# Three ways of feeding TensorE in the gate and up products of a decoder layer: 144-token halves, alternating PSUM tiles, and 256 + 32 tokens

## Chip, cores and metric

The kernel runs on one core of a Trainium2 chip. The metric is the device time of one execution in microseconds (us); lower is better. Two runs of the kernel before gave 2517.14 and 2518.53 us, median 2517.84 us.

## The reference, cut to what matters

One inference step of a decoder layer is computed for a prompt of 256 tokens and for 8 samples of 4 tokens, so 288 tokens go through the same weights. The layer is a half-step feed-forward network (FFN), a mixing stage (a state space model and sparse attention), and a second half-step FFN. Only the first FFN is changed:

```
def _swiglu(x, w_gate, w_up, w_down):
    return (jax.nn.silu(x @ w_gate) * (x @ w_up)) @ w_down
...
x_p = x_p + FFN_RES * _swiglu(_rms_norm(x_p, p['ffn1_norm']), p['ffn1_w_gate'], p['ffn1_w_up'], p['ffn1_w_down'])
```

The model width is 2048 (16 blocks of 128) and the FFN width 5632 (44 blocks of 128). Weights and inputs are float32.

## The kernel before

All activations are kept as tiles of 128 features by 288 tokens. To keep float32's accuracy with single-pass products, every operand is split into an upper part, rounded to the type float32r, and a lower part, the rest, in float32r too. A product of weights and activations is then three matmuls that add up in the same PSUM tile: upper weights by upper activations, upper weights by lower activations, and lower weights by upper activations. The profile prints both types as "f32".

`project` (L221) computes 256 columns of a weight matrix against all 288 tokens. `fetch` (L204) brings in a piece of 512 rows by 256 columns by a DMA on the SP queue into `raw` (4 buffers); `parts` (L211) makes `whi` on ScalarE (L216) and `wlo` on VectorE (L217), 3 buffers each. For each of the two blocks of 128 weight columns there is one PSUM tile, and the loops are: piece of 4 row blocks, then column block j, then row block k, then the three matmuls.

```
            for j in range(m):
                ...
                for k in range(kt):
                    ...
                    nc.tensor.matmul(out, wh, xh, start=k0 + k == 0, stop=False)
                    nc.tensor.matmul(out, wh, xl, start=False, stop=False)
                    nc.tensor.matmul(out, wl, xh, start=False, stop=k0 + k == K - 1)
                    if k % 2:
                        self.tick()
```

These three are L240, L241 and L242. The first matmul operand is the stationary one (the weights in the array), the second streams through it. In every row of these lines in the profile, a LDWEIGHTS on "PEld" goes with a MATMUL on "PE". PSUM tiles come by turns from two pools, so one project's tiles are called `psy` and the next one's `acc`; `hh` and `hl` are the upper and lower parts of the scaled input x, `hi` and `lo` those of the gated product that the down projection takes.

`swiglu` (L340) goes through the FFN width in six groups of 8, 8, 8, 8, 6 and 6 blocks. In a group, `project` is called for gate and for up, two blocks at a time (L359); each resulting PSUM tile is multiplied by 1/rms on VectorE (L372), gate goes through Silu on ScalarE (L374), and gate and up are multiplied and split again (L352, L250). Then 8 calls make the down projection of the group (L380), which VectorE adds to x (L384). A group of 8 blocks has 8 calls for gate and up. Each has 16 row blocks, 2 column blocks and 3 matmuls: 768 matmuls in all.

The order of the instructions on TensorE is that of the program, written by hand. The other engines' orders are made by a scheduler with priorities. Work beside the products (`prepare`, the state space model's matrices) is written as generators that go on a step at each `tick`; in the first FFN its small matmuls and its VectorE work lie among the products of the first four groups. VectorE has both this work and L217 in its queue.

Of the kernel before, what the change touches and what calls it, by code (L numbers as in the profile page):

```python
# [10 lines left out]
F32 = mybir.dt.float32  # L11
# [4 lines left out]
AL = mybir.AluOpType  # L16
AX = mybir.AxisListType

P = 128
SEQ, DB, DT = 256, 8, 4  # L20
# [13 lines left out]
CT = 4  # L34
# [22 lines left out]
def constants():  # L57
    """What depends on the shapes alone."""
    f32 = np.float32
    pos = np.concatenate([np.arange(SEQ), np.tile(PAST + np.arange(DT), DB)]).astype(f32)  # L60

    def rope(rot):
        half = rot // 2
        f = (500000.0 ** (-np.arange(half, dtype=np.float64) * 2.0 / rot)).astype(f32)
        ang = (pos[None, :] * f[:, None]).astype(f32).astype(np.float64)
        c, s = np.cos(ang).astype(f32), np.sin(ang).astype(f32)
        return np.concatenate([c, c]), np.concatenate([-s, s])

    cq, sq = rope(HD // 4)
    ci, si = rope(ID // 4)  # L70
    rope_i = np.zeros((P, 2, NT), f32)
    rope_i[:, 0] = 1.0
    for o in (0, ID):
        rope_i[o:o + ID // 4, 0], rope_i[o:o + ID // 4, 1] = ci, si
    t = np.arange(P)
    causal = np.where(t[None, :] <= t[:, None], 0.0, NEG).astype(f32)
    b, j = np.divmod(np.arange(DB * DT), DT)
    new = np.where((b[:, None] == b[None, :]) & (j[None, :] <= j[:, None]), 0.0, NEG).astype(f32)
    rows = np.zeros((4, DB * DT, 2, 4, 4, HEADS, DT), f32)
    for i in range(DB * DT):  # L80
        for n in range(4):
            rows[n, i, b[i] // 4, n, b[i] % 4, :, j[i]] = 1.0
    strip = np.arange(P) // 32
    same = np.arange(P)[:, None] % 32 == np.arange(P)[None, :] % 32
    strips = np.stack([same, same & (strip[:, None] < strip[None, :])], 1).astype(f32)
    sign = np.where(np.arange(P) // 16 % 2 == 0, 1.0, -1.0).astype(f32)
    pick = np.zeros((P, 34), f32)
    pick[:, 2] = 1.0
    return {
        "c_rope_q": np.stack([cq, sq], 1),  # L90
        "c_rope_i": rope_i,
        "c_causal": causal,
        "c_new": new,
        "c_wmask": (j[:, None] == np.arange(DT)[None, :]).astype(f32),
        "c_rows": rows.reshape(P, 2, 4, P),
        "c_strips": strips,
        "c_sign": sign[:, None],
        "c_pick": pick,
        "c_part": (np.arange(P) % 16).astype(f32)[:, None],
    }  # L100


class Late:
    """A list whose items are made when they are first asked for."""
# [14 lines left out]
class Net:  # L119
# [57 lines left out]
    def pipe(self, n, every, *stages):  # L177
        """n items, one each `every` ticks, through stages (ticks behind the first, what to do)."""
        for t in range((n - 1) * every + max(lag for lag, _ in stages) + 1):
            for lag, fn in stages[::-1]:  # L180
                i, odd = divmod(t - lag, every)
                if not odd and 0 <= i < n:
                    fn(i)
            yield
# [18 lines left out]

    def fetch(self, src, kt, n):  # L204
        """[128 kt, n] of a matrix in DRAM."""
        raw = self.wp.tile([P, 4, 256], F32, tag="raw", bufs=4, name=self.name("raw"))[:, :kt, :n]
        with self.tc.high_priority(offset=FIRST):
            self.nc.sync.dma_start(raw, src.rearrange("(c p) n -> p c n", p=P))
        return raw

    def parts(self, raw):  # L211
        """Its upper and its lower parts."""
# [8 lines left out]
    def project(self, w, c0, n, xs):  # L221
        """PSUM tiles of w[:, c0:c0+n]^T x, of 128 columns of w each (n <= 256)."""
# [23 lines left out]

    def split(self, src):
        nc = self.nc
        hi, lo = self.t(F32R, "hi"), self.t(F32R, "lo")
        nc.scalar.copy(hi, src)  # L250
        nc.vector.tensor_tensor(lo, src, hi.bitcast(F32), op=AL.subtract)
        return hi, lo

# [1 line left out]

    def load_x(self, xp, xs):
        """The inputs, turned as they are asked for."""
# [27 lines left out]
    def rows(self, pool, src):  # L285
        """[n, 128] in DRAM, to be turned."""
# [4 lines left out]
    def turned(self, pool, row, n):  # L291
        """[n, 128] -> [128, n]"""
# [7 lines left out]
    def rsqrt(self, out, m, s):  # L300
        """out = m ** -0.5, the table's root refined by a Newton step; s is scratch."""
# [8 lines left out]
    def normed(self, g):  # L310
        """gain * x, split, and a function that gives the broadcast 1 / rms."""
# [28 lines left out]
    def swiglu(self, pool, i, g, done):  # L340
        nc = self.nc
# [4 lines left out]
        for n in (8, 8, 8, 8, 6, 6):  # L346
# [8 lines left out]
            for j in range(n // 2):  # L355
                c0 = (f0 + 2 * j) * P
                a = []
                for w in (wg, wu):
                    for p in self.project(w, c0, 256, hs):  # L359
# [55 lines left out]

    def exp(self, pool, x, shape):
        """e ** x to float32's accuracy"""
        nc = self.nc
        T = lambda dt=F32: pool.tile(shape, dt, name=self.name("ex"))  # noqa: E731
# [15 lines left out]
    def cos_sin(self, pool, a, shape):  # L435
        nc = self.nc
        T = lambda: pool.tile(shape, F32, name=self.name("cs"))  # noqa: E731
# [19 lines left out]
        # the quadrant, -2 to 2  # L457
# [24 lines left out]
    def prepare(self):  # L482
        """Constants; the SSM's discretization, its matrices and rotations."""
# [12 lines left out]
        dram = lambda name, shape: self.dram.tile(shape, F32, name=name)  # noqa: E731  # L496
# [13 lines left out]
        mul = lambda o, a, b: nc.vector.tensor_tensor(o, a, b, op=AL.mult)  # noqa: E731  # L510
        add = lambda o, a, b: nc.vector.tensor_tensor(o, a, b, op=AL.add)  # noqa: E731
        sub = lambda o, a, b: nc.vector.tensor_tensor(o, a, b, op=AL.subtract)  # noqa: E731

        def states(a):
            """[n, 128] of states, by their parts: [part][n, 4, 16]"""
# [3 lines left out]
        with ExitStack() as outer:  # L519
# [15 lines left out]
            # partition (page, sixteenth of it): where that begins in the caches  # L535
# [11 lines left out]
            # each state's two parts, 16 states a time: [groups, (4, part, 16)]  # L547
            S = [GR, P]
            T = lambda: pool.tile(S, F32, name=self.name("pz"))  # noqa: E731
# [37 lines left out]
            K = lambda shape: keep.tile(shape, F32, name=self.name("pk"))  # noqa: E731  # L587
# [7 lines left out]
            # from here the second factors have their sign by part  # L595
            for a in (sT, fiT):
                nc.vector.tensor_scalar(a, a, sign, None, op0=AL.mult)
            # e ** (i theta n), n a power of two, kept on the unit circle
# [19 lines left out]
            # the decay's powers, 0 to CT, from the first and from the last  # L618
# [19 lines left out]
            # the state that comes in, and that with the decay of a chunk  # L638
# [12 lines left out]
            # b_bar: [states, group, channel]  # L651
# [5 lines left out]
            # c: [(group, channel), states], the imaginary part negative  # L657
# [14 lines left out]
            for c8 in range(8):  # L672
# [16 lines left out]
                def powers(a, a_s, fr, fi, n, op, what):  # L689
                    """[states, group, power, channel]"""  # L690
# [20 lines left out]
                # e ** (i theta CT n)  # L711
# [18 lines left out]
                # what comes out of what comes in 0 to CT - 1 tokens later  # L730
# [13 lines left out]

    def zproj(self, c0, n, hs, scaled=True, tag="t", bufs=N_T):
        """Projections of the normed x, as SBUF tiles of 128 features; not scaled: 1 / rms is still to come."""
# [20 lines left out]
    def chunks(self, z, a):  # L767
        """u: what is left is [channel, place in a chunk, chunk], the samples' chunks first"""
# [5 lines left out]
    def ssm(self, pool, u, za, every):  # L774
        """The state space model: a chunk's inputs to its last state and to its own outputs, a scan of the chunks' states
        (rotated to where the decay is real), and each chunk's outputs from the state before it; four groups a time."""
# [4 lines left out]
        # inputs by group, in zeros where its neighbour's are  # L781
# [43 lines left out]
        def into(n):  # L825
# [16 lines left out]
            flat = lambda a: a.rearrange("p g c -> p (g c)")  # noqa: E731  # L842
# [38 lines left out]
        # the states at the ends  # L881
# [26 lines left out]
    def pages(self, pool, src, i, b, n, tag, bufs):  # L908
        """A sixteenth of a page a partition."""
# [5 lines left out]
    def select(self, qi, kw):  # L915
        """The indexer's inputs; then, for the samples, the bias of the keys each query may see:
        a quarter of the cache in each 32 partitions."""
        nc, D = self.nc, self.D
        with self.tc.tile_pool(name="sel", bufs=1) as pool:
# [24 lines left out]
            # qi is not scaled by 1 / rms: its head weights are instead  # L944
# [5 lines left out]
            # head weights as columns: [(half h t), (half b t)] for each sequence  # L950
# [67 lines left out]
            # the n-th largest of a row, a bit at a time (from the sign down)  # L1018
            one = lambda n, dt=F32: pool.tile([P, 1], dt, name=n)  # noqa: E731
# [19 lines left out]
            # of the equal ones the first: as many as are missing  # L1039
# [9 lines left out]
    def prompt(self, z, out):  # L1049
        """The prompt's selection and attention; the norms of q and k."""  # L1050
# [36 lines left out]
        # head h's sum of squares in partition 32 (h % 4) + h // 4  # L1087
# [76 lines left out]
    def by_token(self, pair, key):  # L1164
        """The two heads of k or v by token, to the outputs too."""
# [18 lines left out]
    def sample(self, z, out):  # L1184
# [4 lines left out]
        with self.tc.tile_pool(name="sample", bufs=1) as pool:  # L1189
# [8 lines left out]
            # queries by sequence, each kv head's in zeros  # L1198
            for h in range(HEADS):
                nc.scalar.copy(qz[:, h // REP, :, h * DT:(h + 1) * DT], q[h][:, SEQ:NT].rearrange("p (b t) -> p b t", t=DT))  # L1200
            for x in range(2):
                # columns: [eighth of the sixteenths, (page, sixteenth)], then the new keys
# [199 lines left out]
```

## Time and profile before

| what | value |
| --- | --- |
| median of the two runs | 2517.84 us |
| span of the profiled execution, first to last instruction | 2517.2 us |
| TensorE's mean granted clock in it (1 is full speed) | 0.999 |
| matmuls, and weight loads, each | 18917 |

The profiled execution's span lies within 0.7 us of the median, so what is outside the span is below a thousandth. In the timelines a MATMUL's duration reaches to its modelled end and overlaps the next one's; the distance from one start to the next is what an instruction costs in a stream. The same holds for LDWEIGHTS. A row of windows gives a stretch and its length, then busy us and number of instructions of PE, PEld, DVE (VectorE), ACT (ScalarE) and POOL (of PE alone where only PE was asked for), then TensorE's granted clock, the DMA engines' busy share and GB/s. In a list of groups the busy us and mean ns stand behind the bar, then the idle time ahead of them and what ended it.

### The profile page before, as it was taken

To read this page: it belongs to the slowest core of one execution; us is meant where nothing else is said; L and a number is where in the kernel's file an instruction comes from. 1 tells how busy PE (TensorE), PEld (TensorE's weight loads), DVE (VectorE), ACT (ScalarE), POOL (GpSimd) and SP (SyncE) were. 2 spreads that over 40 slices of the span, in tenths; PEclk is the share of its full clock that TensorE was granted. 3 is DMA by queue.
4 is the path that set the end of the run, shared out by engine and by line. 5 is a ranking of instruction groups with operands and counts; after the bars stand their busy time and mean duration, and the time that the engine had idled before them with its cause. 6 is when DMAs were issued, how large, how long until landed. Compare 5 with 4: busy or idle time off the path is not lost.

```text
span 2517.2 us, 46484 instructions
## 1 busy us (share of the span) xinstructions
PE 2496.1 (99%) x18917; PEld 2446.9 (97%) x18917; DVE 1529.7 (61%) x2878; ACT 1082.8 (43%) x1600; POOL 98.4 (4%) x116
## 2 busy tenths in 40 slices
PE   8999999999999999999999999999999999999999
PEld 7999999999999998999998999999999999999999
DVE  6658888875555656679644457556555555554555
ACT  5433333333333445445865544344333333333333
POOL 1001000000000000000023210000000000000000
PEclk9999999999999999999999999999999999999999
DMA  6556566565545655446567576555555555555553
GB/s 196 160 160 162 183 195 190 187 184 193 163 154 179 196 170 168 126 133 189 157 216 230 189 244 200 193 167 168 164 164 167 168 168 167 164 166 167 162 174 130
DMA packets 439834, 441.35 MB, mean 175 GB/s; under 512 B 36778, under 2 KB 428964, under 8 KB 439620
## 3 DMA queue, kind: packets, MB, share of 16 engines
q1 hardware_dynamic: 428064, 414.56, 52.3%
q0 software_dynamic: 6688, 20.26, 2.7%
q10 hardware_dynamic: 4868, 3.57, 0.5%
q8 instruction: 148, 2.42, 0.4%
q14 instruction: 66, 0.54, 0.1%
HBM read 418.48 MB, written 19.83 MB: 174 GB/s over the span
## 4 chain that ended last, share of the span: by engine, by line
PE 96%; DMA 1%; DVE 1%; issue 0%; POOL 0%; ACT 0%; POOLq 0%; SPq 0%; ACTq 0%; DVEq 0%
PE acc L240 17%; PE acc L241 17%; PE acc L242 17%; PE psy L240 13%; PE psy L241 13%; PE psy L242 13%; PE aux L1061 1%; PE psy L829 1%; PE aux L1218 1%; PE aux L276 0%; DMA cn<-in_ssm_c_re 0%; DVE wlo L217 0%; PE psy L858 0%; PE aux L1264 0%; PE psy L859 0%
## 5 line engine op out<-in xcount | busy, mean ns | idle before, releaser
L217 DVE TENSOR_TENSOR wlo<-raw,whi 128x1024 fp32r<-128x1024 f32 (+1 forms) x740 | 885.3, 1197 | 754.6 <-ACT whi L216 731.5
L216 ACT CAST whi<-raw 128x1024 fp32r<-128x1024 f32 (+1 forms) x740 | 760.5, 1028 | 1144.4 <-PE acc L241 470.8
L240 PE MATMUL acc<-hh,whi 128*128 128x288 f32 x2240 | 680.3, 304 | 0.0
L242 PE MATMUL acc<-hh,wlo 128*128 128x288 f32 x2240 | 660.6, 295 | 3.1 <-DVE wlo L217 3.1
L241 PE MATMUL acc<-hl,whi 128*128 128x288 f32 x2240 | 661.7, 295 | 0.0
L240 PE MATMUL psy<-hh,whi 128*128 128x288 f32 (+1 forms) x1552 | 465.4, 300 | 0.5 <-DVE g L372 0.3
L241 PE MATMUL psy<-hl,whi 128*128 128x288 f32 (+1 forms) x1552 | 459.5, 296 | 1.2 <-DVE hl L317 1.2
L242 PE MATMUL psy<-hh,wlo 128*128 128x288 f32 (+1 forms) x1552 | 458.6, 295 | 0.0
L240 PEld LDWEIGHTS acc<-hh,whi 128*128 128x128 f32 x2240 | 421.7, 188 | 13.9 <-issue 11.5
L242 PEld LDWEIGHTS acc<-hh,wlo 128*128 128x128 f32 x2240 | 421.8, 188 | 3.6 <-DVE wlo L217 3.6
L241 PEld LDWEIGHTS acc<-hl,whi 128*128 128x128 f32 x2240 | 422.6, 189 | 1.3 <-issue 1.0
L240 PEld LDWEIGHTS psy<-hh,whi 128*128 128x128 f32 (+1 forms) x1552 | 292.2, 188 | 5.5 <-issue 3.9
L241 PEld LDWEIGHTS psy<-hl,whi 128*128 128x128 f32 (+1 forms) x1552 | 293.1, 189 | 2.5 <-DVE hl L317 1.4
L240 PE MATMUL psy<-hi,whi 128*128 128x288 f32 x992 | 293.3, 296 | 0.0
L240 PE MATMUL acc<-hi,whi 128*128 128x288 f32 x992 | 293.3, 296 | 0.0
L241 PE MATMUL acc<-lo,whi 128*128 128x288 f32 x992 | 292.7, 295 | 0.0
L241 PE MATMUL psy<-lo,whi 128*128 128x288 f32 x992 | 292.6, 295 | 0.0
L242 PEld LDWEIGHTS psy<-hh,wlo 128*128 128x128 f32 (+1 forms) x1552 | 292.6, 189 | 0.0
L242 PE MATMUL acc<-hi,wlo 128*128 128x288 f32 x992 | 292.4, 295 | 0.0
L242 PE MATMUL psy<-hi,wlo 128*128 128x288 f32 x992 | 292.3, 295 | 0.0
L240 PEld LDWEIGHTS acc<-hi,whi 128*128 128x128 f32 x992 | 186.3, 188 | 1.4 <-issue 1.2
L240 PEld LDWEIGHTS psy<-hi,whi 128*128 128x128 f32 x992 | 186.3, 188 | 0.7 <-issue 0.4
(403 smaller groups left out, 2351.2 us busy)
## 6 DMA issues: line engine op xcount, KB each, us to landing
raw<-in_ffn_w_gate SPq DMA_DIRECT2D x176, 512.0 KB
raw<-in_ffn_w_up SPq DMA_DIRECT2D x176, 512.0 KB
raw<-in_ffn_w_down SPq DMA_DIRECT2D x160, 512.0 KB
raw<-in_w_in SPq DMA_DIRECT2D x120, 512.0 KB
raw<-in_w_out SPq DMA_DIRECT2D x32, 512.0 KB
raw<-in_ffn_w_down SPq DMA_DIRECT2D x32, 256.0 KB
raw<-in_w_branch_a SPq DMA_DIRECT2D x16, 512.0 KB
raw<-in_w_branch_b SPq DMA_DIRECT2D x16, 512.0 KB
```

The lines of the kernel that those rows point to most:

```text
L216: self.nc.scalar.copy(hi, raw)
L217: self.nc.vector.tensor_tensor(lo, raw, hi.bitcast(F32), op=AL.subtract)
L240: nc.tensor.matmul(out, wh, xh, start=k0 + k == 0, stop=False)
L241: nc.tensor.matmul(out, wh, xl, start=False, stop=False)
L242: nc.tensor.matmul(out, wl, xh, start=False, stop=k0 + k == K - 1)
L829: nc.tensor.matmul(p[:, j * M:(j + 1) * M], I[n][:, j // 2], U[n % 3][:, j // 2, j % 2], start=j == 0, stop=j == 3)
L1061: nc.tensor.matmul(p[:, :L], qi[h // 2][o:o + 64, i * P:(i + 1) * P], kd[o:o + 64, :L], start=True, stop=True)
L1218: nc.tensor.transpose(pk[:, (2 * g + j) * P:(2 * g + j + 1) * P], kr[b4][:, c:c + P], self.ident)
```

## The change

In the first FFN, three of the six groups (blocks 8 to 15, 16 to 23 and 24 to 31, called the second, third and fourth group here) use other forms for gate and up. The second FFN, the down projections and the other groups stay as they are.

- Second group: every matmul is cut in two, tokens 0 to 143 and 144 to 287, with the same stationary operand and into the same PSUM tile.
- Third group: the loop over the two column blocks is the innermost one, so that consecutive matmuls go to the two PSUM tiles by turns and have different weights. The number and shapes of the matmuls stay.
- Fourth group: cut as in the second, but into 256 and 32 tokens.

The rest of the diff removes comments and docstrings.

```
+    def project_cut(self, w, c0, n, xs, cuts):
...
+        for k0 in range(0, K, 4):
+            raw = self.fetch(w[k0 * P:(k0 + 4) * P, c0:c0 + n], 4, n)
+            hi, lo = self.parts(raw)
+            for j in range(2):
+                for k in range(4):
+                    xh, xl = xs[k0 + k]
+                    wh, wl = hi[:, k, j * P:j * P + P], lo[:, k, j * P:j * P + P]
+                    for i, (a, b) in enumerate(((wh, xh), (wh, xl), (wl, xh))):
+                        for c in cuts:
+                            nc.tensor.matmul(acc[j][:, c], a, b[:, c], start=k0 + k + i + c.start == 0,
+                                             stop=k0 + k == K - 1 and i == 2 and c.stop == NT)
+                    if k % 2:
+                        self.tick()
+        return acc
+
+    def project_both(self, w, c0, n, xs):
...
+            for k in range(4):
+                xh, xl = xs[k0 + k]
+                for i, (a, b) in enumerate(((hi, xh), (hi, xl), (lo, xh))):
+                    for j in range(2):
+                        nc.tensor.matmul(acc[j][:, :NT], a[:, k, j * P:j * P + P], b, start=k0 + k + i == 0,
+                                         stop=k0 + k == K - 1 and i == 2)
+                self.tick()
+        return acc
...
                 for w in (wg, wu):
-                    for p in self.project(w, c0, 256, hs):
+                    halves = [slice(0, NT // 2), slice(NT // 2, NT)]
+                    if f0 == 8 and number == 1:
+                        ps = self.project_cut(w, c0, 256, hs, halves)
+                    elif f0 == 16 and number == 1:
+                        ps = self.project_both(w, c0, 256, hs)
+                    elif f0 == 24 and number == 1:
+                        ps = self.project_cut(w, c0, 256, hs, [slice(0, SEQ), slice(SEQ, NT)])
+                    else:
+                        ps = self.project(w, c0, 256, hs)
+                    for p in ps:
```

In `project_cut` and `project_both` the lines ahead of the loops (the turn of the PSUM pools) are as in `project`.

## Rows read from the trace of the kernel before

**Rows 1.** The page: busy us of each engine (part 1), shares of the last chain (part 4).
```profile
PE 2496.1 (99%) x18917; PEld 2446.9 (97%) x18917; DVE 1529.7 (61%) x2878; ACT 1082.8 (43%) x1600; POOL 98.4 (4%) x116
...
PE 96%; DMA 1%; DVE 1%; issue 0%; POOL 0%; ACT 0%; POOLq 0%; SPq 0%; ACTq 0%; DVEq 0%
```

**Rows 2.** Windows: gate and up of the second, third, fourth and fifth group.
```profile
181.29:288.24 106.95, 105.27 (x780) 103.88 (x779) 85.28 (x252) 38.77 (x46) 8.38 (x11) 1.00 0.60 168
342.61:450.20 107.59, 107.59 (x833) 106.79 (x832) 85.98 (x214) 42.23 (x52) 1.46 (x3) 1.00 0.63 192
503.05:608.61 105.56, 105.56 (x811) 105.03 (x810) 71.13 (x152) 41.10 (x50) 4.87 (x6) 1.00 0.63 193
659.84:736.70 76.86, 76.86 (x578) 76.86 (x577) 37.69 (x45) 28.91 (x35) 0.00 (x0) 1.00 0.50 160
```

**Rows 3.** Waits of TensorE, 181 to 609 us: us in total, times, longest.
```profile
PE acc L242 <- DVE wlo L217: 1.7, 1, 1.7
```

**Rows 4.** Page, part 5: weight loads of two lines that share their weights.
```profile
L240 PEld LDWEIGHTS acc<-hh,whi 128*128 128x128 f32 x2240 | 421.7, 188 | 13.9 <-issue 11.5
...
L241 PEld LDWEIGHTS acc<-hl,whi 128*128 128x128 f32 x2240 | 422.6, 189 | 1.3 <-issue 1.0
```

**Rows 5.** Timeline of PEld behind a wait of TensorE: start us, duration us.
```profile
256.25 0.19 PEld L242 LDWEIGHTS acc<-hh,wlo 128*128 128x128 f32 x1 [1.92 <-DVE wlo L217]
256.36 0.19 PEld L240 LDWEIGHTS acc<-hh,whi 128*128 128x128 f32 x1
256.50 0.19 PEld L241 LDWEIGHTS acc<-hl,whi 128*128 128x128 f32 x1
```

**Rows 6.** Timeline of PEld at L829: eight loads, 72 columns streamed by each matmul.
```profile
1035.65 0.97 PEld L829 LDWEIGHTS psy<-U,in 128*128 128x128 f32 x8
1036.54 0.19 PEld L240 LDWEIGHTS acc<-hh,whi 128*128 128x128 f32 x1
```

**Rows 7.** Timeline of PEld at L1235: four loads, 32 columns streamed by each matmul.
```profile
1322.15 0.54 PEld L1235 LDWEIGHTS aux<-z,qz 128*128 128x128 f32 x4
1322.61 0.19 PEld L240 LDWEIGHTS acc<-hh,whi 128*128 128x128 f32 x1
```

**Rows 8.** Timeline of PE, 80 weight columns: first and last of 42 matmuls, and the next.
```profile
942.63 0.30 PE L240 MATMUL psy<-hh,whi 128*80 128x288 f32 x1
...
948.04 0.29 PE L242 MATMUL psy<-hh,wlo 128*80 128x288 f32 x1
948.17 0.29 PE L240 MATMUL acc<-hh,whi 128*128 128x288 f32 x1
```

**Rows 9.** Timeline of PE in the fourth group's stream: first and last of 32 matmuls.
```profile
599.79 0.30 PE L240 MATMUL acc<-hh,whi 128*128 128x288 f32 x1
...
603.92 0.29 PE L241 MATMUL acc<-hl,whi 128*128 128x288 f32 x1
```

**Rows 10.** Timeline of PEld at L1156, plain float32 operands, 256 columns streamed.
```profile
1261.12 0.75 PEld L1156 LDWEIGHTS aux<-pt,vt 128*128 128x128 f32 x4
1261.90 0.19 PEld L240 LDWEIGHTS acc<-hh,whi 128*128 128x128 f32 x1
1262.12 0.19 PEld L241 LDWEIGHTS acc<-hl,whi 128*128 128x128 f32 x1
```

**Rows 11.** Windows of PE alone, around a wait of TensorE for a DMA.
```profile
1373.00:1376.40 3.40, 3.40 (x25) 1.00 0.90 257
1376.40:1379.80 3.40, 1.14 (x10) 1.00 0.84 273
1379.80:1383.20 3.40, 3.40 (x18) 0.51 0.86 304
```

**Rows 12.** Timeline of PE at the lower clock: two consecutive matmuls.
```profile
1382.16 0.44 PE L240 MATMUL acc<-hh,whi 128*128 128x288 f32 x1
1382.40 0.44 PE L241 MATMUL acc<-hl,whi 128*128 128x288 f32 x1
```

More of the change, by code (lines that the diff above doesn't have):

```diff
@@ L245, in project @@
         return acc
+    def project_cut(self, w, c0, n, xs, cuts):
+        nc = self.nc
+        K = len(xs)
+        self.turn = self.wide and not self.turn
+        acc = [self.py() if self.turn else self.ps() for _ in range(2)]
+        for k0 in range(0, K, 4):
[13 more added lines that the diff above has]
+    def project_both(self, w, c0, n, xs):
+        nc = self.nc
+        K = len(xs)
+        self.turn = self.wide and not self.turn
+        acc = [self.py() if self.turn else self.ps() for _ in range(2)]
+        for k0 in range(0, K, 4):
+            raw = self.fetch(w[k0 * P:(k0 + 4) * P, c0:c0 + n], 4, n)
+            hi, lo = self.parts(raw)
+            for k in range(4):
[6 more added lines that the diff above has]
+        return acc
     def split(self, src):
@@ L340, in swiglu @@
     def swiglu(self, pool, i, g, done):
+        number = i
         nc = self.nc
```

## The prediction, made before the changed kernel ran

> **What bounds the kernel now.** I read the page first. TensorE is busy for 2496.1 of 2517.2 us, and 96% of the chain that ended last is TensorE's own work; VectorE, the next engine, has 61% [rows 1]. So a change of the matmul stream counts at full price, unless it fills or opens a wait. Next I read the three changed stretches by windows, and the fifth group beside them [rows 2]. The clock is at full speed, 2.4 GHz, in all four. In the fifth group nothing else lies among the products: 576 matmuls take 76.86 us, which is 133.4 ns for one. At that rate 768 take 102.5 us; the changed groups take 106.95, 107.59 and 105.56 us, so 3.1 to 5.1 us of each is side work and waits. Of waits the list has one over half a microsecond there: 1.7 us in the second group, for `wlo` from VectorE [rows 3], which is busy for 85.28 of 106.95 us in that group.
>
> The question is then what makes up the 133.4 ns. Three readings answer most of it.
> - A weight load is paid for by every matmul. L240 and L241 use the same part of `whi`, one right behind the other, and each has as many loads as the other [rows 4]. Nothing here skips a load because the weights are already in the array. Both halves of a cut matmul will load the same 128 columns again.
> - A load of 128 columns takes about 111 ns, and the next one can't start earlier. Behind the wait, the second load starts 0.11 us after the first, when the array had nothing to stream [rows 5]. At L829 eight loads with only 72 columns streamed by each take 1036.54 - 1035.65 = 0.89 us, so 111 ns each [rows 6]; at L1235, with 32 columns, four take 0.46 us, 115 ns each, of which the first still stands behind a stream of its predecessor [rows 7].
> - The load is not what sets 133.4 ns: with 80 weight columns in place of 128, 41 distances make 5.41 us, 132 ns [rows 8], the same as the 31 distances of 133 ns with 128 columns [rows 9]. So 288 columns streamed set it, and today's load hides under them with 20 ns to spare.
>
> **The change, part by part.** The second group's halves stream 144 columns each. By share that is 67 ns, shorter than the load. The two matmuls and two loads then cost two loads, 2 x 111 = 222 ns, where one matmul cost 133.4. L829 is the nearest row: float32 weights of 128 columns and 72 columns streamed. It is plain float32, whose columns cost more, as rows 10 show (0.22 us for 256), so 72 of them stream for some 61 ns, much like 144 here. Group two: 768 x (222 - 133.4) = +68.0 us. From below, two loads at 109 ns give +65 us. From above, nothing in the trace runs pairs of load and matmul faster than 133.4 ns for more than a handful, so 2 x 133.4 is the far end: +102.5 us. I take 111 ns, from the row nearest in shape.
>
> The fourth group's 256 tokens stream for 133.4 x 256 / 288 = 118.6 ns, which hides the load for the 32 that follow. The 32 tokens then stream for some 15 ns, and the load for the next 256 starts only when the 32 are in the array: 111 ns. Together 229.6 ns; 768 x (229.6 - 133.4) = +73.9 us. The bounds are +65 (both at 109 ns) and +102.5 us.
>
> The third group has as many loads and matmuls of the same shapes as before, in other order. A change of PSUM tile occurs in the trace too: the step from a `psy` tile to an `acc` tile takes 0.13 us like all its neighbours [rows 8], so neither a gain nor a cost is seen. It can't gain more than 768 x (133.4 - 120) = 10.3 us, since 288 columns at 2.4 GHz take 120 ns, and the same row's rounding, 0.14 us, would be a loss of 5 us. I take 0. `wlo` is asked for by the fifth matmul of a piece in place of the third, which is later and so safe; both PSUM tiles end together, which is 12 matmuls or 1.6 us later for the first of them, and the down projection asks for the last gated pair only 30 matmuls on, some 4 us. If that cover fails, it costs about 1 us once.
>
> The rest is free or small. The DMAs, `whi`, `wlo` and the evacuations are as many as before, and the same ticks lie between the same pieces, so the side work keeps its places. Both slower groups give VectorE and the DMA queue more time: the 1.7 us wait should go, -1.7 us. The 1536 additional matmuls and loads wait for nothing and nobody waits for them alone. No engine becomes late next: VectorE's 85 us lie in some 173 us then.
>
> Sum: 68.0 + 73.9 + 0 - 1.7 = +140.2 us on the profiled span of 2517.2, so 2657.4 us. The median of the runs lies 0.7 us above the span: **2658 us**, 5.6% slower. About 2% is what a measurement of this kernel tells from no change.
>
> **The rivals.**
> - *The weights stay, or their load costs no time* (the side that is not slower). If a second load of the weights that are already there were hidden, two halves would cost their columns, 2 x 67 = 133.4 ns, and 256 + 32 the same; the change would be nothing but 768 matmuls more per group. At 13.4 ns each, the whole of what 133.4 is above 120, that is +21 us: 2516 to 2537 us. It decides if a repeated load takes under 133.4 / 2 = 67 ns. Rows 4 count such loads without telling their time, since a 288-column stream covers them; rows 6 and 7 are against it, though with other weights each time. Chance 0.06. The Trainium skill's "TensorE: Matmul & The Clock Gate", section "Back-to-back issue gap", has a rule by which a warm matmul of N columns takes N / 2.4 + 2.5 ns. By that rule a half takes 62.5 ns, the change gives back some 8 ns a pair and the time is 2503 us. Where it can be held against this trace it is low: 122.5 ns for 288 columns, and the rows have 133.
> - *TensorE's issue sets the pace.* If a pair of load and matmul can't be issued in less than today's 133.4 ns over a long stretch, two halves cost 266.8 ns and so do 256 + 32: +205 us, 2721 us. For it: the runs at less are short, eight pairs in rows 6 and four in rows 7. Against it: behind the 1.7 us wait, in which instructions had time to queue, the matmuls go on at the same distance [rows 5], and 80-column weights change nothing. Chance 0.11. [...]
> - *Short float32r streams fall to the price of plain float32.* A plain float32 product is two instructions: the four at L1156 are two products of the program. One with 256 columns takes 1262.12 - 1261.90 = 0.22 us, 0.85 ns a column [rows 10], since a load starts as the matmul ahead of it does. A half would then take 2 x 122 = 245 ns, the pair 489, +273 us; the 32 tokens two loads, 222 ns, the pair 341, +159 us: in all some 2950 us. For it: the trace has no float32r matmul under 256 columns. Against it: the 288-column ones stay far under plain float32's price, and nothing in rows 8 or 9 hints at a second mode. Chance 0.09.
> - *The clock falls.* With loads as the bound, the array streams for only some 60% of the second group. The clock fell once in the trace, behind 3.4 us of which TensorE was busy for 1.14 [rows 11], and 288 columns took 0.24 us then [rows 12]. At half clock a pair of halves takes 240 ns if loads keep their pace (+82 us, within the range) and 444 if they don't (+239 us, the time 2829 or more). A long stretch bound by loads is not in the trace. Chance of the latter 0.03.
>
> **How the numbers follow.** The forecast, loads at 109 to 120 ns in both cut groups, has 0.66; the rivals have 0.06, 0.11, 0.09 and 0.03, and 0.05 is left for what I don't see, most of it slower. The range takes in the bounds of the forecast and the issue rival. Low: 2517.8 + 65 + 65 - 10.3 - 1.7 = 2636. High: 2517.8 + 205 + 5 = 2728. Outside lie the kept weights, plain float32 and the fallen clock, 0.18. Under 2467 us, faster by 2%, none of the cases comes: 0.01. Within 2% is the first rival alone, 0.06; slower has 0.93.
>
> **What would show it.** Windows of the second group should have about 173 us, the third 107.6 and the fourth 179, at clock 1.00. In the second group's timeline loads should start every 0.11 us; in the fourth the distances should alternate between 0.12 and 0.11. TensorE should have 1536 more of both kinds, and no new waits. Distances of 0.07 would speak for the first rival, 0.13 in both halves for issue, 0.24 for plain float32 or the clock, which the windows' clock column tells apart. If the third group moves by more than 10 us, my reading of the PSUM tiles is wrong.

## The result, and the profile after

The changed kernel takes 2659.57 us (2658.11 to 2661.03, two runs), 1.0563 times the time before, with a 95% interval of 1.0546 to 1.058. The forecast was 2658 us, range 2636 to 2728.

First the page of the changed kernel, engines and last chain, against [rows 1]:

```profile
PE 2639.8 (99%) x20453; PEld 2591.6 (98%) x20453; DVE 1535.3 (58%) x2878; ACT 1084.0 (41%) x1600; POOL 96.5 (4%) x116
...
PE 98%; DMA 1%; DVE 1%; issue 0%; ACT 0%; SPq 0%; ACTq 0%; DVEq 0%
```

There are 1536 more matmuls and 1536 more loads, and TensorE has the chain even more to itself. Next the windows of the second, third, fourth and fifth group's gate and up, which answer to [rows 2]:

```profile
180.90:354.56 173.66, 173.66 (x1548) 172.94 (x1547) 89.78 (x255) 39.72 (x47) 8.39 (x11) 1.00 0.38 108
408.96:516.93 107.97, 107.97 (x833) 107.16 (x832) 85.25 (x212) 42.10 (x53) 1.45 (x3) 1.00 0.64 192
570.02:749.87 179.85, 179.85 (x1580) 179.57 (x1578) 74.17 (x152) 42.03 (x52) 4.12 (x6) 1.00 0.38 116
800.71:877.59 76.88, 76.88 (x578) 76.88 (x577) 37.67 (x45) 28.86 (x35) 0.00 (x0) 1.00 0.51 161
```

The whole result is in the second column. The halves take 173.66 us in place of 106.95 (+66.7), the 256 + 32 tokens 179.85 in place of 105.56 (+74.3), the PSUM tiles by turns 107.97 in place of 107.59 (+0.4), and the unchanged fifth group 76.88 in place of 76.86. Together that is +141.4 us; the span grew by 2656.3 - 2517.2 = 139.1. The 2.3 us between lie outside these windows, and only part of them is traced: a wait in the mixing stage for gathered keys is 1.1 us long where it was 2.3, and a second wait for `wlo`, of 1.4 us and ahead of the second group, is gone. Against that, TensorE ran at half clock for a few us twice, from 34 and from 1123 us, and in the kernel before once, from 1380 us. The wait of [rows 3] for `wlo` is gone: the second group's TensorE is busy for all of its 173.66 us, where 1.7 were missing. VectorE's work is nearly the same (89.78 us busy in place of 85.28), and the DMA engines' work is spread thinner (share 0.38 in place of 0.60).

The pace itself is in the timeline of PEld in the second group, loads merged by two:

```profile
249.89 0.30 PEld L262 LDWEIGHTS acc<-hh,whi 128*128 128x128 f32 x2
250.12 0.30 PEld L262 LDWEIGHTS acc<-hl,whi 128*128 128x128 f32 x2
250.34 0.30 PEld L262 LDWEIGHTS acc<-hh,wlo 128*128 128x128 f32 x2
```

Two loads start every 0.22 to 0.23 us, 111 ns each, one behind the other as at L829 in [rows 6]: TensorE loads all the time. In the fourth group, timelines of PE and of PEld:

```profile
649.84 0.38 PE L262 MATMUL acc<-hh,wlo 128*128 128x256 f32 x2
650.07 0.38 PE L262 MATMUL acc<-hh,whi 128*128 128x256 f32 x2
```

```profile
649.81 0.30 PEld L262 LDWEIGHTS acc<-hh,wlo 128*128 128x128 f32 x2
650.04 0.30 PEld L262 LDWEIGHTS acc<-hh,whi 128*128 128x128 f32 x2
650.27 0.30 PEld L262 LDWEIGHTS acc<-hl,whi 128*128 128x128 f32 x2
```

A pair takes 0.23 us (650.07 - 649.84, 650.27 - 650.04). The merged rows also say where inside it the second one starts: a load's record lasts 0.19 us, two end 0.30 us after the first began, so the second began 0.11 us in and the next pair 0.12 us later.

### The profile page after: what moved, and what is told of

Same layout as the page of the kernel before. It is cut to its first block, busy times and chain, and to the rows that moved or that the text cites. A ratio compares the mean times of both kernels' runs of the same rounds, so it can differ in the third digit from the quotient of the medians.

```text
span 2656.3 us, 49552 instructions
## 1 busy us (share of the span) xinstructions
PE 2639.8 (99%) x20453; PEld 2591.6 (98%) x20453; DVE 1535.3 (58%) x2878; ACT 1084.0 (41%) x1600; POOL 96.5 (4%) x116
## 4 chain that ended last, share of the span: by engine, by line
PE 98%; DMA 1%; DVE 1%; issue 0%; ACT 0%; SPq 0%; ACTq 0%; DVEq 0%
PE acc L240 14%; PE acc L241 14%; PE acc L242 14%; PE psy L240 11%; PE psy L241 11%; PE psy L242 11%; PE psy L262 7%; PE acc L262 7%; PE acc L281 2%; PE psy L281 2%; PE aux L1110 1%; PE psy L878 1%; PE aux L1267 0%; PE psy L907 0%; PE psy L908 0%
## 5 line engine op out<-in xcount | busy, mean ns | idle before, releaser
L240 PE MATMUL acc<-hh,whi 128*128 128x288 f32 x1856 | 566.3, 305 | 0.0
L241 PE MATMUL acc<-hl,whi 128*128 128x288 f32 x1856 | 548.2, 295 | 0.0
L242 PE MATMUL acc<-hh,wlo 128*128 128x288 f32 x1856 | 547.0, 295 | 0.0
L240 PEld LDWEIGHTS acc<-hh,whi 128*128 128x128 f32 x1856 | 349.4, 188 | 13.5 <-issue 11.5
L241 PEld LDWEIGHTS acc<-hl,whi 128*128 128x128 f32 x1856 | 350.5, 189 | 1.5 <-issue 1.1
L240 PE MATMUL psy<-hh,whi 128*128 128x288 f32 (+1 forms) x1168 | 351.1, 301 | 0.5 <-DVE g L421 0.3
L242 PEld LDWEIGHTS acc<-hh,wlo 128*128 128x128 f32 x1856 | 349.6, 188 | 0.0
L241 PE MATMUL psy<-hl,whi 128*128 128x288 f32 (+1 forms) x1168 | 346.3, 296 | 1.5 <-DVE hl L356 1.5
L242 PE MATMUL psy<-hh,wlo 128*128 128x288 f32 (+1 forms) x1168 | 345.7, 296 | 0.0
L241 PEld LDWEIGHTS psy<-lo,whi 128*128 128x128 f32 x992 | 186.7, 188 | 0.2 <-DVE lo L290 0.2
```

## Experiments

**The theory:** every matmul loads its weights anew, a load of 128 float32r columns takes 111 ns, and a matmul costs the longer of its own stream and the load for the next one. The rivals differ in what the 111 ns hang on: a floor of short matmuls or of issuing (1), the streamed columns (2), loading the same weights again (3), the PSUM tile (4). Kernels were run once with a profile, beside one run or more of the kernel before on the same chip, which took 2514 to 2522 us; the fourth was timed in rounds. All changes are in gate and up of the first FFN unless said otherwise.

### Fewer weight columns

```
+    m = P if k0 + k + i == 0 or k0 + k + i == K + 1 else cols
+    for c in cuts:
+        nc.tensor.matmul(acc[j][:m, c], a[:, k, j * P:j * P + m], b[:, c], ...)
...
 second group: cuts [0:144, 144:288], cols 64
 third group:  cuts [0:288], cols 64
 fourth group: cuts [0:96, 96:192, 192:288], cols 32
```

> Leaves out: in the second, third and fourth group of the first FFN all products but the first and the last of a PSUM tile use only the first 64 (fourth group: 32) of a block's 128 weight columns, so most of the upper rows of these tiles are missing. Second group: halves of 144 tokens by 64 weight columns. Third: all 288 tokens by 64 weight columns. Fourth: thirds of 96 tokens by 32 weight columns. Theory (a matmul waits for its own weight load, priced by the weight columns, 111 ns for 128): the loads take some 56 and 28 ns and hide again, the streams set the pace at 0.42 to 0.46 ns a column. Second group 1536 x 67 to 73 ns, 106 to 116 us; third 107 to 108 us; fourth 2304 x 45 to 53 ns, 106 to 126 us. Rival 1 (111 ns is a floor of any short float32r matmul, or of issuing a load and a matmul, whatever the weights): second group 174 us, third 108, fourth 2304 x 111 ns, 259 us.

The run took 2527.45 us. Windows of the three groups:

```profile
180.70:291.58 110.88, 109.30 (x1549) 108.21 (x1547) 85.40 (x253) 38.80 (x47) 8.38 (x11) 1.00 0.59 163
347.55:453.65 106.10, 106.10 (x833) 105.13 (x832) 85.57 (x214) 42.10 (x52) 1.46 (x3) 1.00 0.65 195
506.49:620.05 113.56, 113.56 (x2348) 113.22 (x2346) 70.97 (x151) 41.30 (x51) 4.54 (x6) 1.00 0.58 180
```

and the timelines of PE within the second and the fourth:

```profile
239.83 0.30 PE L261 MATMUL psy<-hh,wlo 128*64 128x144 f32 x2
239.96 0.30 PE L261 MATMUL psy<-hh,whi 128*64 128x144 f32 x2
240.10 0.29 PE L261 MATMUL psy<-hl,whi 128*64 128x144 f32 x2
240.23 0.30 PE L261 MATMUL psy<-hh,wlo 128*64 128x144 f32 x2
```

```profile
559.86 0.30 PE L261 MATMUL acc<-hl,whi 128*32 128x96 f32 x3
560.00 0.30 PE L261 MATMUL acc<-hh,wlo 128*32 128x96 f32 x3
560.14 0.29 PE L261 MATMUL acc<-hh,whi 128*32 128x96 f32 x3
```

With 64 weight columns two halves take 0.13 to 0.14 us, what the whole takes: cutting the stream is then free. With 32 columns three thirds do the same, 0.14 us. Rival 1 falls, both as a floor and as the pace of issuing: a pair of load and matmul can follow the one ahead after 46 ns, all through a group of 2304 pairs. The first and the last product of each of a group's 16 tiles keep 128 weight columns. In the second group these 32 products cost two loads each as in the changed kernel, 32 x (222 - 133.4) = 2.8 us, most of the 3.9 us that its window is above that of before; in the fourth they cost three, 32 x (333 - 133.4) = 6.4 of 8.0 us. The middle window, 1.5 us shorter than before, confirms that 128-column loads do no more than a trace of harm under a 288-column stream. In the second group the wait for `wlo` is back (1.6 us of the window without TensorE), as the group is almost as fast as before again.

### Other cuts

```
 second group: [0:96, 96:192, 192:288]
 third group:  [0:240, 240:288]
 fourth group: [0:272, 272:288]
```

> Other cuts of the 288 tokens, all weights as they are. Second group 96 + 96 + 96, third 240 + 48, fourth 272 + 16. Theory (each matmul costs the longer of its stream and the load behind it, 111 ns): second 3 x 111 = 333 ns for 133.4, 256 + 3 = 259 us; third 111 + 111 = 222 ns, 171 + 5 = 176 us; fourth 126 + 111 = 237 ns, 182 + 3 = 185 us. Rival 2 (streams under 256 columns run at 0.77 ns a column, which is 111 for 144 too): second 3 x 74 = 222 ns, 174 us; third 185 + 111 = 296 ns, 232 us; fourth about as the theory.

The run took 3046.25 us, far above what the theory (2818 us for the sum) or rival 2 gives. Windows: the start and the rest of the second group, the down projection behind it, then the third and the fourth group:

```profile
181.19:187.00 5.81, 5.81 (x55) 5.81 (x54) 1.68 (x2) 1.05 (x1) 0.00 (x0) 1.00 0.62 183
190.50:669.40 478.90, 478.90 (x2244) 477.95 (x2243) 89.69 (x253) 38.75 (x47) 8.37 (x11) 0.50 0.13 37
673.00:725.26 52.26, 52.26 (x411) 51.73 (x410) 41.18 (x112) 18.01 (x19) 0.99 (x2) 1.00 0.57 178
725.26:901.62 176.36, 176.36 (x1601) 175.94 (x1600) 93.69 (x224) 43.09 (x53) 1.46 (x3) 1.00 0.40 122
954.49:1139.66 185.17, 185.17 (x1579) 184.89 (x1578) 74.07 (x153) 42.09 (x52) 4.54 (x6) 1.00 0.37 113
```

The last two rows are the theory's numbers, 176 and 185 us, and 232 us for the third group is gone with rival 2. The second row is the surprise, and the column ahead of the DMA share explains it: the granted clock is 0.50, 1.2 GHz, through all of that row, and 1.00 in the first 5.81 us of thirds ahead of it and in the down projection behind it. The expectation had no such case. The timeline of PEld at the fall, loads merged by three:

```profile
187.10 0.42 PEld L262 LDWEIGHTS psy<-hh,whi 128*128 128x128 f32 x3
187.44 0.42 PEld L262 LDWEIGHTS psy<-hl,whi 128*128 128x128 f32 x3
187.77 0.65 PEld L262 LDWEIGHTS psy<-hh,wlo 128*128 128x128 f32 x3
188.30 0.76 PEld L262 LDWEIGHTS psy<-hh,whi 128*128 128x128 f32 x3
188.94 0.76 PEld L262 LDWEIGHTS psy<-hl,whi 128*128 128x128 f32 x3
```

Ahead of the fall three loads take 0.33 to 0.34 us, 111 ns each, as the theory has it for thirds; behind it 0.64, 213 ns each. So the load follows the clock. The Trainium skill's "TensorE: Matmul & The Clock Gate", section "LDWEIGHTS (loading the stationary operand)", gives the load of P columns as P / 1.2 ns, 107 ns for 128: the 111 at full clock are near it, the 213 at half clock are not, and the section names no clock.

### Halves with other weights in turn, and half the tokens left out

```
+    for k in range(4):
+        for i, (a, b) in enumerate(((hi, xh), (hi, xl), (lo, xh))):
+            for c in halves:
+                for j in range(2):
+                    nc.tensor.matmul(acc[j][:, c], a[:, k, j * P:j * P + P], b[:, c], ...)
...
 fourth group, in project's order: c = slice(0, NT if k0 + k + i == 0 else NT // 2)
```

> Second group: halves of 144 tokens with the two column blocks by turns, so that no matmul loads the weights that the one ahead of it loaded. Fourth group: only the first 144 tokens are computed (all 288 in a tile's first product alone), which leaves out most of the other half's products. Third group as before. Theory (a load costs the same whatever was loaded before; a 144-token matmul costs 111 ns even with half the work gone): second group 174 us as with equal weights, fourth 768 x 111 ns + 3 = 88 us. Rival 3 (the price is that of loading the same weights again): second group 768 x 133.4 + 3, 106 us. Rival for the fourth (a stream's cost alone): 768 x 67 ns + 3 = 54 us.

The run took 2570.02 us. Windows of the second and the fourth group:

```profile
181.47:355.15 173.68, 173.68 (x1549) 172.95 (x1547) 87.42 (x252) 39.21 (x47) 8.37 (x11) 1.00 0.38 108
569.98:659.32 89.34, 89.34 (x812) 88.96 (x810) 68.69 (x151) 40.52 (x50) 4.83 (x6) 1.00 0.74 227
```

173.68 us with other weights each time, 173.66 with the same: what was loaded before plays no part, and rival 3 falls. In the fourth group half of the streamed columns are gone, and only 16 us of 105.56 with them: each of the 768 matmuls still costs some 112 ns, (89.34 - 3) / 768.

### PSUM tiles by turns everywhere

```
-    if f0 == 8 and number == 1: ...
+    if f0 or number == 2:
+        ps = self.project_both(w, c0, 256, hs)
```

> The third group's form, PSUM tiles by turns, in all groups of both FFNs but the very first: 7680 matmuls in place of 768, no cuts anywhere. Theory (the order of PSUM tiles costs and gives nothing): 2518 us, within 0.2% of before; at the 0.4 us that the third group grew by in the changed kernel it would be +4 us. Rival 4 (two matmuls in a row into one tile cost part of what 133.4 ns is above 120): up to 13.4 ns x 7680, 103 us faster; at 1 ns each 7.7 us faster.

2518.55 us, 1.0003 times the kernel before, interval 0.9992 to 1.0015. Of the 103 us that rival 4 could have given, the interval leaves room for 2, and for a loss of 4 us. Windows of the third and the fifth group, which answer to [rows 2]:

```profile
342.56:450.53 107.97, 107.97 (x834) 107.16 (x832) 85.38 (x212) 42.19 (x53) 1.46 (x3) 1.00 0.63 192
660.83:737.55 76.72, 76.72 (x578) 76.72 (x577) 36.20 (x43) 28.48 (x35) 0.00 (x0) 1.00 0.51 161
```

The third group has the same +0.4 us as in the changed kernel, the fifth is 0.14 us shorter.

### Operands read as bfloat16

```
+    up = lambda a: a.bitcast(BF16)[:, 1::2]
...
-    xh, xl = xs[k0 + k]
+    xh, xl = (up(a) for a in xs[k0 + k])
     (the weights likewise)
 second group: halves; third: all 288; fourth: 256 + 32
```

> Leaves out: in the second, third and fourth group of the first FFN each operand of the gate and up products is read as bfloat16, the upper 16 bits of its float32r value, from the same tiles with a step of two elements. Second group: halves of 144 tokens; third: all 288; fourth: 256 + 32. Theory (111 ns is the load of 128 columns of a 4-byte type; the bfloat16 loads of the kernel before start far closer): the halves hide their loads, 2 x 62 to 67 ns, second group 99 to 106 us; third 94 to 103 + 5, 99 to 108 us; fourth 107 to 119 and 25 to 35 ns, 104 to 121 us. Rival (a load costs 111 ns whatever the type): second group 174 us, third 99 to 108, fourth 171 to 180 us. The third group also tells whether what 133.4 ns is above 120 belongs to float32r: 122 to 124 ns in its distances if so, 133 if not.

The run took 2521.13 us. Windows of the three groups:

```profile
182.99:288.04 105.05, 102.26 (x1548) 100.71 (x1547) 85.06 (x252) 38.71 (x46) 8.39 (x11) 1.00 0.62 172
344.12:446.92 102.80, 102.80 (x834) 78.22 (x832) 84.59 (x212) 41.61 (x52) 1.38 (x3) 1.00 0.66 199
499.85:610.60 110.75, 110.75 (x1579) 97.05 (x1578) 71.54 (x152) 40.87 (x50) 4.54 (x6) 1.00 0.59 185
```

Timeline of PE in the second:

```profile
239.87 0.29 PE L263 MATMUL psy<-hh,whi 128*128 128x144 bf16 x2
240.00 0.29 PE L263 MATMUL psy<-hl,whi 128*128 128x144 bf16 x2
240.13 0.29 PE L263 MATMUL psy<-hh,wlo 128*128 128x144 bf16 x2
```

Two halves take 0.13 us with all 128 weight columns. So the load's 111 ns belong to the 4-byte type, and halves of bfloat16 operands are free. The third group tells that the whole stream isn't quite alike: 102.80 us for 107.59, that is 6 ns less for a matmul, about half of what 133.4 is above 120, and neither of the two values expected. The reads take every second element, and whether the type or that step sets the 127 ns isn't shown. Nor is every cut free: with 256 + 32 tokens the fourth group is 8 us above the third, some 0.14 us for a pair.

### Thirds again, thirds between full streams, and 128 + 160 tokens

```
 second group: [0:96, 96:192, 192:288]
 third group:  for c in (thirds if k % 2 else [slice(0, NT)])
 fourth group: [0:128, 128:288]
```

> Second group: thirds of 96 tokens again. Third: thirds of 96 for every other row block, all 288 tokens for the blocks between. Fourth: 128 + 160 tokens. Nothing is left out. Theory (in the earlier run with thirds the clock fell to half because of what the thirds leave TensorE to stream, and the loads fell with it, 111 to 213 ns): the second group falls again, 2304 x 213 ns, 490 us at a clock of about 0.5; the third, which streams full tokens in between, keeps clock 1.00 and the prices of 111 and 133 ns, 384 x (333 + 133.4) + 5 = 184 us; the fourth keeps it too, 768 x 222 + 3 = 174 us. Rival 5 (the low clock of that run came from elsewhere): the second group takes 259 us. Rival 6 (any long stretch bound by loads loses the clock sooner or later): the third takes 384 x (639 + 240) + 5 = 343 us and the fourth 768 x 426 + 3 = 330 us.

The run took 3050.36 us. Windows of the three groups:

```profile
180.89:672.03 491.14, 491.14 (x2316) 490.10 (x2315) 91.44 (x255) 40.42 (x48) 8.36 (x11) 0.50 0.13 39
728.18:912.24 184.06, 184.06 (x1602) 183.58 (x1600) 93.94 (x226) 43.18 (x54) 1.46 (x3) 1.00 0.39 118
965.10:1139.81 174.71, 174.71 (x1580) 174.33 (x1578) 74.27 (x153) 42.05 (x51) 3.99 (x6) 1.00 0.39 120
```

All three windows fall where the theory puts them, 490, 184 and 174 us. The low clock comes back with the thirds (rival 5 falls), and not with every stretch bound by loads (rival 6 falls): with full streams in between, or in 128 + 160, the clock is 1.00 and a load costs 111 ns. This also tells the two costs of thirds apart: 259 us would be the loads' at full clock, 491 are with the clock's.

## Why the prediction was right

- **What bounds the kernel** held: all of the change came out at TensorE's price, and nothing else became late.
- **Halves:** 68.0 us for the loads and -1.7 for the wait, +66.3; measured +66.7. The price of 111 ns came from L829 [rows 6], whose streams of some 61 ns leave the loads as exposed as 144 tokens do. That it holds for 1536 matmuls on end was an assumption, and the issue rival its price if wrong; the narrow weights show pairs at 46 ns, so there was ample room. The trace of the kernel before could have told as much: it is not so that nothing in it runs pairs below 133.4 ns for more than a handful. At L858 and L859 sixteen loads of 72 columns, each with its matmul, take 1064.27 - 1063.24 = 1.03 us, 64 ns each (timeline of PEld, the first of eight rows merged by two, and the load behind them):

```profile
1063.24 0.20 PEld L858 LDWEIGHTS psy<-chunk,U 128*72 128x72 f32 x2
...
1064.27 0.19 PEld L240 LDWEIGHTS acc<-hh,whi 128*128 128x128 f32 x1
```

  So the issue rival's 0.11 was too much for what was on record; these rows also fit a load that goes by its columns.
- **256 + 32:** +73.9 us, measured +74.3. The loads alternate as forecast, 0.11 and 0.12 us. I said it of "the distances" in general, and for matmuls it is wrong: a merged pair of MATMULs in the fourth group ends 0.38 us after it began, so the second one, of 32 columns and 177 ns long at the least, began 0.20 us in, and the next pair follows 0.03 us later. That fits a MATMUL's record that begins when the array is done with the one ahead, not when its own weights are there. The pair's sum is the same; single distances in a stretch bound by loads are to be read on PEld.
- **PSUM tiles by turns:** 0 forecast, +0.4 us measured, and no effect beyond the interval over ten times as many matmuls. (The first tile of a pair ends 11 matmuls later, not 12, which changes nothing.)
- **The wait for `wlo`** went as forecast, and came back in the first experiment, where the group was fast again. The cover for the last gated pair of the third group held: TensorE has no wait there.
- **The rivals:** kept weights and free reloads are shown wrong by the halves themselves and by the turns with other weights. Issue is shown wrong by 46 ns pairs. A plain-float32 price for short streams is shown wrong by 240 + 48, 96 and 144 columns. The clock rival is the one that was real, with the right price for its worse case (I put 444 ns for two halves; two loads at half clock take 426), only not at this cut: thirds of 128 weight columns throughout lost the clock in both runs of them, halves in none. That halves would keep it could not be read from the rows of before, as the prediction says itself ("A long stretch bound by loads is not in the trace"). So the 0.03 rested on no row that shows such a stretch, and in this the forecast was lucky: one cut further, at 96 tokens, the loads alone would have given 259 us and the group took 491.

## What to carry to other kernels

Before cutting a float32r matmul's moving operand, hold the pieces against the weight load that every matmul pays again: 111 ns for 128 weight columns here, the time of some 240 streamed tokens, so that every cut of 288 tokens that was tried lost, while with 64 weight columns or bfloat16 operands the same halves were free or nearly so. The order of PSUM tiles gave and cost nothing in such a stream. Where loads set the pace, look at the granted clock of the stretch as well, since with 96-token pieces it halved, and the loads with it.

## What the runs showed of the hardware that was not expected

The clock fell to 0.50 in a stretch in which TensorE had no wait at all: 478.90 us of 478.90 busy, with loads of 128 columns behind one another and 96 columns streamed by each. It fell 6.7 us after the thirds began, in the second run of them 3.5 us after, and rose soon after the full streams of the down projection had begun. What in the thirds lowers it isn't shown: loads back to back alone don't, as 144 columns, 128 + 160 and 240 + 48 kept 1.00. Thirds with 32 weight columns, pairs of 46 ns, kept 1.00. The Trainium skill's "TensorE: Matmul & The Clock Gate", section "Why this matters for your kernels", asks for no idle gaps between bursts to keep the clock; here the profile shows no gap, and busy by the profile was not enough.

What makes 288 columns take 133 ns and not 120 is only narrowed down: not the load (64 weight columns took off 1.5 us of 107.59 in a group), not the PSUM tile, and hardly a fixed cost of each matmul (halves and thirds with narrow weights take the same 0.13 to 0.14 us together). It goes with the columns streamed, the bfloat16 reads have about half of it, and at half clock it was gone, 0.24 us for 288 columns [rows 12]. What it is stays open.
